# Expert weights with two neighbouring rows to a partition

## Chip, cores and metric

One core of one Trainium2 chip runs the whole program. The metric is the device time of one execution in microseconds (us). The kernel before takes 1276.35 us (median of 3 runs, 1276.34 to 1277.07).

## What is computed

A hybrid layer on 256 tokens and 16 meta tokens of width 1024, all in float32: a layer norm, an attention branch and a state-space branch, gates, an output projection, a second layer norm, a mixture of 32 experts (each token goes to its 4 best), and a last layer norm. The change lies in the experts:

```python
t = h.reshape(-1, dm)
logits = (t @ w_router + b_router).astype(jnp.float32)
top_v, top_i = lax.top_k(logits, TOP_K)
top_w = jax.nn.softmax(top_v, axis=-1)
comb = jnp.einsum('tk,tke->te', top_w, jax.nn.one_hot(top_i, N_EXPERTS, dtype=jnp.float32))
out = jnp.zeros(t.shape, jnp.float32)
for e in range(N_EXPERTS):
    gate = jnp.minimum(t @ w_gate[e] + b_gate[e], SWIGLU_LIMIT)
    up = jnp.clip(t @ w_up[e] + b_up[e], -SWIGLU_LIMIT, SWIGLU_LIMIT)
    act = (up + 1.0) * gate * jax.nn.sigmoid(SWIGLU_ALPHA * gate)
    out = out + comb[:, e:e + 1] * (act @ w_down[e] + b_down[e])
```

Each of `w_gate[e]`, `w_up[e]` and `w_down[e]` is a 1024 x 1024 matrix of 4 MiB, so the experts' weights are 384 MiB, and each is read once.

## The kernel before

The front (up to about 280 us) computes the norm, the two branches, the gates and the router. The experts follow in 16 pairs. For a pair, `gather` picks up to 64 tokens of each of the two experts by a product with a 0/1 matrix (`gather_mm`, line 908: the normed tokens `z1` are the stationary operand), and `affine` (line 848) puts the first norm's gain and bias on the result, which becomes `XT`, 8 tiles of 128 features. `gate_up` (line 1003) multiplies `XT` with the gate and up matrices, 64 columns of the array for each half of the output. `activate` makes the activation, `act_T` (line 1033) transposes it 128 features at a time into `aT`, and `down` (line 1041) multiplies with `w_down` for both experts side by side. `combine` (line 1057) adds the pair's result to the 256 tokens.

A weight matrix comes in quarters of 256 rows, 1 MiB each. `expert_load` (line 705) puts a quarter into a slot of 128 partitions x 2048 floats. Partition p of it takes row p and row 128 + p of the quarter: two pieces of 4096 B, 512 KiB apart in memory. `part_load` (line 701) loads the last two quarters of `w_down` in halves. There are 21 slots of 1 MiB in all for them; `homes` lists which load takes which.

The orders of PE (TensorE) and SP (which issues the loads) are the program's own, written out by hand; the other engines' orders come from a scheduler outside the stretches marked by hand. A load is issued when the slot that it takes has been read for the last time, so SP waits for PE, and PE waits for the transfers. In the front, rows of small parameters are loaded one above the other (`prow`, `prow2`) and transposed by PE into columns (`pcol`, `pcol2`), so that each partition has its feature's gain and bias.

A branch for experts with over 64 tokens (from line 1118 on) isn't taken with these inputs.

Of the kernel before, what the change touches and what calls it, by code (L numbers as in the profile page):

```python
# [9 lines left out]
F32 = mybir.dt.float32  # L10
# [4 lines left out]
AF = mybir.ActivationFunctionType  # L15
ALU = mybir.AluOpType
# [4 lines left out]
P = 128  # L21
D = 1024
KD = D // P
SEQ = 256
# [24 lines left out]
def hybrid_trunk_kernel(ctx: ExitStack, tc: tile.TileContext, x, meta, ln_in_g, ln_in_b, w_in, b_f,  # L49
# [3 lines left out]
    nc = tc.nc  # L53
    V, S, G, TE = nc.vector, nc.scalar, nc.gpsimd, nc.tensor

    def bc(ap, axis, n):
        a = ap.unsqueeze(axis)
        shape = list(a.shape)
        shape[axis] = n
        return a.broadcast_to(shape)  # L60
# [5 lines left out]
    keep = ctx.enter_context(tc.tile_pool(name="keep", bufs=1))  # L66
# [5 lines left out]
    sp = scan.enter_context(tc.tile_pool(name="sp", bufs=1, side="right"))  # L72
# [6 lines left out]
    def pst(cols, dt=F32, rows=P):  # L79
        t = ps.tile([P, 512], F32, name="ps", tag="ps")  # L80
        return t[:rows, :cols]
# [5 lines left out]
    ident = const.tile([P, P], F32, name="ident")  # L87
    make_identity(nc, ident)
    R_ARE, R_AIM, R_L1G, R_L1B, R_L2G, R_L2B, NROW = 16, 32, 48, 56, 64, 72, 80
    R_BGLU, R_D, R_BF, NROW2 = 0, 4, 8, 9  # L90
    prow0 = sp.tile([P, P], F32, name="prow0", tag="y", bufs=1)
    prow = sp.tile([P, P], F32, name="prow")
    prow2 = sp.tile([P, P], F32, name="prow2", tag="ya", bufs=1)
    ldt = sp.tile([16, 2], F32, name="ldt")

    def slab(src, kt):
# [27 lines left out]
    G.memset(prow2[:NROW2], 0.0)  # L124
    nc.sync.dma_start(prow2[R_BGLU:R_BGLU + 4], b_glu.rearrange("l (k p) -> (l k) p", p=P))
    nc.sync.dma_start(prow2[R_D:R_D + 4], ssm_d.rearrange("l (q g) c -> (l q) (g c)", g=8))
    nc.sync.dma_start(prow2[R_BF:R_BF + 1].rearrange("o (a b) -> o a b", b=32)[:, :, :NH], bc(b_f, 1, 4))
    ctt = ap_.tile([P, 2, 4, NS], F32, name="ctt", tag="vmz")
    ct = [ctt[:, i] for i in range(2)]
# [66 lines left out]
    pcol0 = sp.tile([P, 16], F32, name="pcol0")  # L196
    pcol = keep.tile([P, NROW], F32, name="pcol")
    pcol2 = keep.tile([P, 16], F32, name="pcol2")
    hT = fk.tile([P, KD, T], F32, name="hT", tag="hT")

    def col(r, n=1):
        return pcol[:, r:r + n]
# [18 lines left out]
    with tc.manual_schedule(engines={ENG.DVE, ENG.Activation, ENG.Pool}):  # L221
        for t_ in (wfp, bz, Mz, qA, kA):
            G.memset(t_, 0.0)
        G.tensor_scalar(prow[0:16].rearrange("j (g p) -> j g p", g=2), bc(ldt, 2, NS), 1.0, 1.0,
                        op0=ALU.mult, op1=ALU.mult)
        pp = pst(16)
# [15 lines left out]
        for n in range(2):  # L242
# [3 lines left out]
                            op0=ALU.mult, op1=ALU.add)  # L246
        for k in range(KD):
            pt = pst(T)
# [8 lines left out]
        pt = project(wu, 0, 0, T)  # L257
        pp = pst(NROW)
# [3 lines left out]
    pp = pst(NROW2)  # L262
    TE.transpose(pp, prow2[:NROW2], ident[:NROW2, :NROW2])
    S.copy(pcol2[:, :NROW2], pp)
    with tc.issue_after(xn.ins):
        mark = u_tile(1)
    with tc.issue_after(mark.ins):
# [117 lines left out]
    for i in range(2):  # L385
# [4 lines left out]
        pt = pst(512)  # L390
# [307 lines left out]

    home = homes()

    def part_load(t_, w, e, qtr, k):
        r = 256 * qtr + 128 * k
        nc.sync.dma_start(t_[:, k], w[0, e, r:r + 128])

    def expert_load(w, e, qtr, load=True):
        key = (w.tensor.name, e, qtr)
        if key in ready:
            return ready.pop(key)
        pool, tag = home[nload[0]]
        nload[0] += 1  # L710
        t_ = pools[pool].tile([P, 2048], F32, name="w", tag=tag).rearrange("p (k n) -> p k n", n=D)
        if load:
            nc.sync.dma_start(t_, w[0, e, qtr * 256:qtr * 256 + 256].rearrange("(k p) n -> p k n", p=P))
        return t_

    def prefetch(n):
# [128 lines left out]
    XT = xy[:, 0]  # L845
    Ysb = xy[:, 1].rearrange("p k n -> p (k n)")

    def affine(k, out_, in_):
        if k % 2:
            V.tensor_scalar(out_, in_, col(R_L1G + k), col(R_L1B + k), op0=ALU.mult, op1=ALU.add)  # L850
        else:
            S.activation(out_, in_, AF.Identity, scale=col(R_L1G + k), bias=col(R_L1B + k))  # L852

    def transposed(i):
        z1T[i] = xy[:, 1] if i else fk.tile([P, KD, P], F32, name="z1T", tag="y2T")
# [51 lines left out]

    def gather_mm(pts, sel, i):
        for k in range(KD):
            TE.matmul(pts[k // 4][:, (k % 4) * P:(k % 4 + 1) * P], z1[:, i, k * P:(k + 1) * P],  # L910
                      sel[:, i].rearrange("p e s -> p (e s)"), start=i == 0 and k % 4 == 0, stop=i == 1,
                      skip_group_check=True)

# [119 lines left out]
    def act_T(up):  # L1033
        pt = px.tile([P, 512], F32, name="px", tag="px")
        for j in range(4):
            TE.transpose(pt[:, j * P:(j + 1) * P], up[:, j * P:(j + 1) * P], ident)  # L1036
        aT = mp.tile([P, 4, 2, CAP], F32, name="aT", tag="aT", bufs=2)
        S.copy(aT.rearrange("p j h s -> p (j h s)"), pt)  # L1038
        return aT
# [78 lines left out]
    with tc.If(anyc > CAP):  # L1118
        free = [s_ for s_ in slots if s_ != ("keep", "gate1")]
        for s_ in home[-8:]:  # L1120
            free.remove(s_)
        free.sort(key=lambda s_: ("wC", "fk", "wB", "wA").index(s_[0]))

        def slot(n):
            pool, tag = free[n]
            return pools[pool].tile([P, 2048], F32, name="w", tag=tag)

        h1Td = slot(0).rearrange("p (k t) -> p k t", k=KD)
        for k in range(KD):
            pt = px.tile([P, 512], F32, name="px", tag="px")  # L1130
            for i in range(2):
                TE.transpose(pt[:, i * P:(i + 1) * P], z1[:, i, k * P:(k + 1) * P], ident)
            affine(k, h1Td[:, k], pt[:, :SEQ])
        with tc.For_i(0, NE, 1) as e:
            ce = nc.values_load(cnti[0:1, bass.ds(e, 1)], min_val=0, max_val=SEQ)
            with tc.If(ce > CAP):
                def weights_of(w, n):
                    ts = []
                    for qtr in range(4):
                        ts.append(slot(n + qtr).rearrange("p (k n) -> p k n", n=D))  # L1140
                        nc.sync.dma_start(ts[-1], w[0, bass.ds(e, 1), qtr * 256:qtr * 256 + 256]
                                          .rearrange("o (k p) n -> p (o k) n", p=P))
                    return ts

                scr = slot(1)
                a, sg, br, bu = scr[:, 0:512], scr[:, 512:1024], scr[0:1, 1024:], scr[32:33, 1024:]
                nc.sync.dma_start(br, b_gate[0, bass.ds(e, 1), :])
                nc.sync.dma_start(bu, b_up[0, bass.ds(e, 1), :])
                aT = slot(2).rearrange("p (k t) -> p k t", k=KD)
                wg_e, wu_e = weights_of(w_gate, 3), weights_of(w_up, 7)  # L1150
                for i in range(2):
                    for n in range(2):
                        ns = slice(n * 512, n * 512 + 512)
                        pts = []
                        for ws, bb_, r, tag in ((wg_e, br, 0, "pg"), (wu_e, bu, 32, "pu")):
                            pt = pg.tile([P, 512], F32, name=tag, tag=tag)
                            TE.matmul(pt, ones[r:r + 1, 0:P], bb_[:, ns], start=True, stop=False)
                            for k in range(KD):
                                TE.matmul(pt, h1Td[:, k, i * P:(i + 1) * P], ws[k // 2][:, k % 2, ns],
                                          start=False, stop=k == KD - 1)  # L1160
                            pts.append(pt)
                        V.tensor_scalar_min(a, pts[0], 7.0)
                        S.activation(sg, a, AF.Sigmoid, scale=1.702)
                        V.tensor_mul(sg, sg, a)
                        V.tensor_scalar(a, pts[1], 7.0, -7.0, op0=ALU.min, op1=ALU.max)
                        V.scalar_tensor_tensor(a, a, 1.0, sg, op0=ALU.add, op1=ALU.mult)
                        pt = px.tile([P, 512], F32, name="px", tag="px")
                        for j in range(4):
                            TE.transpose(pt[:, j * P:(j + 1) * P], a[:, j * P:(j + 1) * P], ident)
                        V.tensor_copy(aT[:, 4 * n:4 * n + 4, i * P:(i + 1) * P],  # L1170
                                      pt.rearrange("p (k t) -> p k t", k=4))
                wd_e = weights_of(w_down, 7)
                for i in range(2):
                    for n in range(2):
                        ns = slice(n * 512, n * 512 + 512)
                        pt = px.tile([P, 512], F32, name="px", tag="px")
                        for k in range(KD):
                            TE.matmul(pt, aT[:, k, i * P:(i + 1) * P], wd_e[k // 2][:, k % 2, ns],
                                      start=k == 0, stop=k == KD - 1)
                        V.scalar_tensor_tensor(acc[:, i, ns], pt, over[:, i, bass.ds(e, 1)], acc[:, i, ns],  # L1180
                                               op0=ALU.mult, op1=ALU.add)
# [81 lines left out]
```

## Time and profile before

| | us |
|---|---|
| median of 3 runs | 1276.35 |
| the profiled execution | 1274.92 |
| its span, from the first to the last instruction | 1273.2 |
| PE (matmul) busy | 1175.0 (92%) |
| PE weight loads busy | 573.8 (45%) |
| DVE busy | 328.8 (26%) |
| ACT busy | 169.1 (13%) |
| bytes moved by DMA | 433.09 MB, 340 GB/s over the span |

Busy time is the union of an engine's instructions. Matmuls are pipelined and their ends are modelled, so 92% for PE isn't 92% of its peak. The mean of 340 GB/s hides two stages: the front, which moves less, and the experts, where the loads run on without a break.

### The profile page before, as it was taken

The numbers are of one execution on the slowest core, as the hardware profiler recorded it, in microseconds if no ns is written. First come the engines' busy times: TensorE is split into PE (matmuls) and PEld (weight loads), VectorE is DVE, ScalarE is ACT, GpSimd is POOL, SyncE is SP. The second block draws the span as 40 slices with busy tenths as digits, with TensorE's granted clock in tenths as the row PEclk, the third lists the DMA queues.
The fourth block names the chain that finished last, engine by engine and source line by source line (L and its number), as shares of the span: only waits on it lengthen the run. The fifth ranks groups of instructions, "written<-read, shape, count | busy, mean of one in ns | idle before, by whom it ended". The sixth has DMA issues, their size and how long they took to land. (4 is left out here: it accounts for less than half of the span.)

```text
span 1273.2 us, 13451 instructions
## 1 busy us (share of the span) xinstructions
PE 1175.0 (92%) x5508; PEld 573.8 (45%) x5509; DVE 328.8 (26%) x784; ACT 169.1 (13%) x380; POOL 58.7 (5%) x115
## 2 busy tenths in 40 slices
PE   4889999989999999999999999999999999999965
PEld 2777888653434343344434343533434242424221
DVE  3969410241141212021111212121211111111103
ACT  2357201020101010010101010110101010101010
POOL 3324200000000000000000000000000000000001
PEclk9999999989989999999999999999999999999988
DMA  7651399459978999999999999999999999999970
GB/s 155 168 120 47 131 268 350 190 184 410 369 309 355 409 410 409 410 408 409 408 409 409 409 409 409 409 409 409 408 409 409 409 409 409 409 409 409 409 293 33
DMA packets 124507, 433.09 MB, mean 340 GB/s; under 512 B 14162, under 2 KB 14506, under 8 KB 124442
## 3 DMA queue, kind: packets, MB, share of 16 engines
q1 hardware_dynamic: 124010, 431.66, 88.4%
q8 instruction: 45, 0.74, 0.2%
q10 hardware_dynamic: 432, 0.52, 0.1%
q14 instruction: 20, 0.16, 0.0%
HBM read 431.11 MB, written 1.05 MB: 339 GB/s over the span
## 5 line engine op out<-in xcount | busy, mean ns | idle before, releaser
L1050 PE MATMUL Yp<-w,aT 128*64 128x512 f32 x1024 | 242.6, 606 | 10.9 <-PEq L1118 5.8
L1015 PE MATMUL pg<-w,xy 128*64 128x512 f32 x1024 | 239.7, 595 | 4.9 <-DMA w<-in_w_gate_dram 4.5
L1015 PE MATMUL pu<-w,xy 128*64 128x512 f32 x1024 | 231.5, 597 | 8.8 <-DMA w<-in_w_up_dram 8.4
L1050 PEld LDWEIGHTS Yp<-w,aT 128*64 128x64 f32 x1024 | 105.2, 139 | 134.4 <-issue 117.5
L1015 PEld LDWEIGHTS pg<-w,xy 128*64 128x64 f32 x1024 | 85.8, 137 | 145.7 <-issue 124.6
L1015 PEld LDWEIGHTS pu<-w,xy 128*64 128x64 f32 x1024 | 68.7, 136 | 168.6 <-issue 133.4
L210 PE MATMUL ps<-hT,w 128*128 128x256 f32 (+1 forms) x512 | 119.7, 393 | 2.8 <-ACT pr L587 2.8
L210 PEld LDWEIGHTS ps<-hT,w 128*128 128x128 f32 x512 | 98.3, 194 | 19.8 <-ACT pr L587 3.1
L1026 DVE TENSOR_SCALAR pg<-pg 128x512 f32<-128x512 f32 x32 | 22.4, 700 | 249.0 <-PE pg L1019 249.0
L1027 ACT ACTIVATE ups<-pg 128x512 f32<-128x512 f32 x32 | 19.1, 597 | 466.9 <-DVE pg L1026 466.9
L1029 DVE TENSOR_SCALAR pu<-pu 128x512 f32<-128x512 f32 x32 | 22.4, 700 | 208.3 <-PE pu L1019 208.3
L1053 DVE COPY xy<-Yp 128x512 f32<-128x512 f32 x16 | 11.1, 692 | 248.5 <-PE Yp L1050 248.5
L1061 PE MATMUL px<-xy,selT 128*128 128x512 f32 x120 | 61.2, 635 | 2.9 <-DVE acc L1062 2.9
L910 PE MATMUL px<-sel,z 128*128 128x128 f32 x480 | 57.6, 278 | 0.6 <-DVE sel L915 0.6
L910 PEld LDWEIGHTS px<-sel,z 128*128 128x128 f32 x480 | 55.8, 192 | 1.2 <-ACT aT L1038 0.8
L1213 POOL TENSOR_TENSOR acc<-acc,gb 128x512 f32<-128x512 f32 (+1 forms) x2 | 2.0, 994 | 1103.5 <-ACT acc L1211 1103.5
L1062 DVE TENSOR_TENSOR acc<-acc,px 128x512 f32<-128x512 f32 x60 | 39.8, 683 | 13.6 <-PE px L1061 13.6
L1054 ACT COPY xy<-Yp 128x512 f32<-128x512 f32 x16 | 9.4, 586 | 244.9 <-PE Yp L1050 244.9
L1061 PEld LDWEIGHTS px<-xy,selT 128*128 128x128 f32 x120 | 21.0, 195 | 43.6 <-issue 22.1
L1038 ACT COPY aT<-px 128x512 f32<-128x512 f32 x32 | 18.8, 587 | 127.5 <-PE px L1036 127.5
L850 DVE TENSOR_SCALAR xy<-px,pcol 128x128 f32<-128x128 f32 x60 | 23.6, 409 | 42.7 <-ACT xy L852 40.9
L1019 PE MATMUL pg<-bias,ident 32*64 32x512 f32 x128 | 34.3, 612 | 0.0
(349 smaller groups left out, 803.8 us busy)
## 6 DMA issues: line engine op xcount, KB each, us to landing
w<-in_w_gate_dram SPq DMA_DIRECT2D x128, 1024.0 KB, 13.0
w<-in_w_up_dram SPq DMA_DIRECT2D x128, 1024.0 KB, 18.3
w<-in_w_down_dram SPq DMA_DIRECT2D x126, 1024.0 KB, 18.3
w<-in_w_in_dram SPq DMA_DIRECT2D x16, 1024.0 KB, 16.2
w<-in_w_o_dram SPq DMA_DIRECT2D x4, 1024.0 KB
w<-in_w_up_a_dram SPq DMA_DIRECT2D x2, 1024.0 KB
w<-in_w_up_b_dram SPq DMA_DIRECT2D x2, 1024.0 KB
w<-in_w_down_dram SPq DMA_DIRECT2D x4, 512.0 KB, 15.7
```

What stands on the lines that cost most here:

```text
L210: TE.matmul(pt, w[k][:, j * P:(j + 1) * P], hT[:, k, n0:n1], start=k == 0, stop=k == KD - 1)
L850: V.tensor_scalar(out_, in_, col(R_L1G + k), col(R_L1B + k), op0=ALU.mult, op1=ALU.add)
L910: TE.matmul(pts[k // 4][:, (k % 4) * P:(k % 4 + 1) * P], z1[:, i, k * P:(k + 1) * P], sel[:, i].rearrange("p e s -> p (e s)"), start=i == ...
L1015: TE.matmul(pt[64 * n:64 * n + 64], XT[:, kk, c0:c0 + CAP], wt[:, k, n * 512:n * 512 + 512], start=kk == 0, stop=False, skip_group_check=True)
L1019: TE.matmul(pt[64 * n:64 * n + 64], ident[bs, NE * j + e:NE * j + e + 1].broadcast_to([NE, CAP]), bias[bs, n * 512:n * 512 + 512], start=F ...
L1026: V.tensor_scalar_min(pgt, pgt, 7.0)
L1027: S.activation(up, pgt, AF.Sigmoid, scale=1.702)
L1029: V.tensor_scalar(put, put, 7.0, -7.0, op0=ALU.min, op1=ALU.max)
L1038: S.copy(aT.rearrange("p j h s -> p (j h s)"), pt)
L1050: TE.matmul(Yp[n][64 * g:64 * g + 64], aTs[g][:, j, half], wd[g][:, k, n * 512:n * 512 + 512], start=qtr == 0 and k == 0, stop=qtr == 3 an ...
L1061: TE.matmul(pt, selT[:, i * P:(i + 1) * P], Ysb[:, ns], start=True, stop=True)
L1062: V.tensor_add(acc[:, i, ns], acc[:, i, ns], pt)
```

## The change

A slot now holds two neighbouring rows to a partition: partition p takes rows 2p and 2p + 1 of the quarter, 8192 B in one piece. So tile k of `XT` and of `aT` has to hold the features 256 (k // 2) + k % 2 + 2p. `paired(k)` gives that slice, of stride 2, and it is now the stationary operand in `gather_mm` and `act_T`, where 128 neighbouring columns stood before. `affine` needs gain and bias in the new order: two more small loads (`prowP`), two small transposes and a copy make `pcolP`. In the branch that isn't taken the old order is kept (`natural=True`).

```diff
+    prowP = sp.tile([8, 256], F32, name="prowP")
...
     nc.sync.dma_start(prow2[R_D:R_D + 4], ssm_d.rearrange("l (q g) c -> (l q) (g c)", g=8))
+    for j, a in enumerate((ln1_g, ln1_b)):
+        nc.sync.dma_start(prowP[4 * j:4 * j + 4], a.rearrange("l (q n) -> (l q) n", n=256))
     nc.sync.dma_start(prow2[R_BF:R_BF + 1].rearrange("o (a b) -> o a b", b=32)[:, :, :NH], bc(b_f, 1, 4))
...
+    pcolP = keep.tile([P, 16], F32, name="pcolP")
...
     S.copy(pcol2[:, :NROW2], pp)
+    pp = pst(16)
+    for k in range(2):
+        TE.transpose(pp[:, 8 * k:8 * k + 8], prowP[:, k::2], ident[:8, :8])
+    S.copy(pcolP, pp)
...
     def part_load(t_, w, e, qtr, k):
-        r = 256 * qtr + 128 * k
-        nc.sync.dma_start(t_[:, k], w[0, e, r:r + 128])
+        nc.sync.dma_start(t_[:, k], w[0, e, 256 * qtr:256 * qtr + 256].rearrange("(p k) n -> k p n", k=2)[k])
...
         if load:
-            nc.sync.dma_start(t_, w[0, e, qtr * 256:qtr * 256 + 256].rearrange("(k p) n -> p k n", p=P))
+            nc.sync.dma_start(t_, w[0, e, qtr * 256:qtr * 256 + 256].rearrange("(p k) n -> p k n", k=2))
...
-    def affine(k, out_, in_):
+    def paired(k):
+
+        return slice(256 * (k // 2) + k % 2, 256 * (k // 2) + 256, 2)
+
+    def affine(k, out_, in_, natural=False):
+        if natural:
+            g_, b_ = col(R_L1G + k), col(R_L1B + k)
+        else:
+            c = 8 * (k % 2) + k // 2
+            g_, b_ = pcolP[:, c:c + 1], pcolP[:, c + 4:c + 5]
         if k % 2:
-            V.tensor_scalar(out_, in_, col(R_L1G + k), col(R_L1B + k), op0=ALU.mult, op1=ALU.add)
+            V.tensor_scalar(out_, in_, g_, b_, op0=ALU.mult, op1=ALU.add)
         else:
-            S.activation(out_, in_, AF.Identity, scale=col(R_L1G + k), bias=col(R_L1B + k))
+            S.activation(out_, in_, AF.Identity, scale=g_, bias=b_)
...
     def gather_mm(pts, sel, i):
         for k in range(KD):
-            TE.matmul(pts[k // 4][:, (k % 4) * P:(k % 4 + 1) * P], z1[:, i, k * P:(k + 1) * P],
+            TE.matmul(pts[k // 4][:, (k % 4) * P:(k % 4 + 1) * P], z1[:, i, paired(k)],
...
-            TE.transpose(pt[:, j * P:(j + 1) * P], up[:, j * P:(j + 1) * P], ident)
+            TE.transpose(pt[:, j * P:(j + 1) * P], up[:, paired(j)], ident)
```

No instruction of the old program changes its place. On SP, among the experts, a pair's loads stand before as pieces of 2 x 1024 floats to a partition:

```order
L713 DMA w<-in_w_gate_dram 128x2x1024 x4
L713 DMA w<-in_w_up_dram 128x2x1024 x4
L713 DMA w<-in_w_gate_dram 128x2x1024 x4
L713 DMA w<-in_w_up_dram 128x2x1024 x4
L713 DMA w<-in_w_down_dram 128x2x1024 x8
```

and now in the same order, as one piece of 2048 floats:

```order
L721 DMA w<-in_w_gate_dram 128x2048 x4
L721 DMA w<-in_w_up_dram 128x2048 x4
L721 DMA w<-in_w_gate_dram 128x2048 x4
L721 DMA w<-in_w_up_dram 128x2048 x4
L721 DMA w<-in_w_down_dram 128x2048 x8
```

Only the shape differs. On SP in the front, between the small parameter loads (`prow_90` is `prow2`) and the first loads of the state-space branch, there stands before:

```order
L125 DMA prow_90<-in_b_glu_dram 4x128
L126 DMA prow_90<-in_ssm_d_dram 4x128
L127 DMA prow_90<-in_b_f_dram 1x4x8
L131 DMA ctt<-in_ssm_c_re_dram 128x4x64
L131 DMA ctt<-in_ssm_c_im_dram 128x4x64
```

and now:

```order
L126 DMA prow_90<-in_b_glu_dram 4x128
L127 DMA prow_90<-in_ssm_d_dram 4x128
L129 DMA prowP<-in_ln_g_dram 4x256
L129 DMA prowP<-in_ln_b_dram 4x256
L130 DMA prow_90<-in_b_f_dram 1x4x8
L134 DMA ctt<-in_ssm_c_re_dram 128x4x64
L134 DMA ctt<-in_ssm_c_im_dram 128x4x64
```

So everything from `b_f` on is issued two loads later. On PE, after the first projection of the front, there stands before:

```order
L210 MATMUL ps<-hT,w 128x272 x8
L259 MATMUL ps<-ident,prow 128x80
L263 MATMUL ps<-ident,prow_90 128x9
L210 MATMUL ps<-hT,w 128x272 x8
L392 MATMUL ps<-ident,cz 128x128 x8
```

and now:

```order
L214 MATMUL ps<-hT,w 128x272 x8
L263 MATMUL ps<-ident,prow 128x80
L267 MATMUL ps<-ident,prow_90 128x9
L271 MATMUL ps<-ident,prowP 128x8 x2
L214 MATMUL ps<-hT,w 128x272 x8
L400 MATMUL ps<-ident,cz 128x128 x8
```

Two small transposes come in ahead of the second projection.

## Rows read from the trace of the kernel before

**Rows 1.** The page: span, PE's busy time, and clock and DMA in 40 slices.

```profile
span 1273.2 us, 13451 instructions
...
PEclk9999999989989999999999999999999999999988
DMA  7651399459978999999999999999999999999970
GB/s 155 168 120 47 131 268 350 190 184 410 369 309 355 409 410 409 410 408 409 408 409 409 409 409 409 409 409 409 408 409 409 409 409 409 409 409 409 409 293 33
```

**Rows 2.** Windows, one per expert pair: start:end us, engines' busy us, PEclk, DMA share, GB/s.

```profile
408.60:466.20 57.60, 55.84 (x261) 22.75 (x259) 11.12 (x19) 5.05 (x10) 0.00 (x0) 1.00 1.03 409
...
523.80:583.20 59.40, 57.64 (x262) 25.79 (x260) 11.31 (x20) 5.05 (x10) 0.00 (x0) 0.97 1.03 409
...
872.60:930.40 57.80, 56.03 (x262) 22.73 (x260) 11.11 (x19) 5.05 (x10) 0.00 (x0) 1.00 1.03 409
930.40:991.80 61.40, 57.19 (x262) 21.77 (x260) 11.11 (x19) 5.05 (x10) 0.00 (x0) 1.00 1.03 409
...
1114.90:1177.60 62.70, 57.49 (x261) 21.45 (x260) 10.75 (x18) 5.05 (x10) 0.00 (x0) 1.00 1.03 409
...
930.40:1177.60 247.20, 229.22 (x1035) 86.07 (x1033) 44.09 (x75) 20.20 (x40) 0.00 (x0) 1.00 1.03 409
408.60:1222.00 813.40, 776.92 (x3543) 313.75 (x3539) 151.46 (x257) 69.76 (x137) 0.00 (x0) 1.00 1.03 409
```

**Rows 3.** Waits, whole run: engine line <- releaser: us, times, longest.

```profile
PEld pu L1015 <- DMA w<-in_w_up_dram: 33.7, 33, 1.5
```

**Rows 4.** Waits from 930 us to the end.

```profile
PEld pu L1015 <- DMA w<-in_w_up_dram: 31.6, 29, 1.5
```

**Rows 5.** Timeline, PE in a late pair: start us, us, instruction, idle before.

```profile
1006.61 1.94 PE L1015 MATMUL pu<-w,xy 128*64 128x512 f32 x8 [0.62 <-DMA w<-in_w_up_dram]
```

**Rows 6.** Waits of SP, the queue that issues the loads, whole run.

```profile
SPq L713 <- PE pg L1015: 179.2, 92, 20.5
SPq L713 <- PE Yp L1050: 152.4, 78, 13.7
```

**Rows 7.** Windows in the front and in the experts, columns as in rows 2.

```profile
28.00:32.00 4.00, 4.00 (x17) 3.07 (x17) 0.97 (x8) 1.05 (x2) 0.00 (x0) 1.00 1.04 161
39.00:43.00 4.00, 3.86 (x12) 3.22 (x13) 4.00 (x21) 0.89 (x2) 0.53 (x1) 0.58 1.05 397
40.00:41.00 1.00, 1.00 (x5) 0.77 (x4) 1.00 (x6) 0.59 (x1) 0.00 (x0) 0.50 1.07 406
42.00:43.00 1.00, 1.00 (x5) 0.79 (x4) 1.00 (x7) 0.00 (x0) 0.00 (x0) 0.81 1.06 408
500.00:504.00 4.00, 4.00 (x24) 1.52 (x21) 0.71 (x2) 0.11 (x1) 0.00 (x0) 1.00 1.02 409
```

**Rows 8.** Timeline, SP in the front.

```profile
23.43 25.66 SPq L103 DMA_DIRECT2D w<-in_w_in_dram  x6
```

**Rows 9.** Timeline, PE's weight loads at a pair's transposes and gather.

```profile
735.15 0.42 PEld L1036 LDWEIGHTS px<-ident,ups 128*128 128x128 f32 x4 [0.81 <-issue]
735.54 3.76 PEld L910 LDWEIGHTS px<-sel,z 128*128 128x128 f32 x32
```

**Rows 10.** Timeline, PE in the front: a matmul whose moving operand has stride 2.

```profile
100.45 0.49 PE L507 MATMUL ps<-uT,Mz 128*128 128x128 f32 x2
100.78 0.62 PE L210 MATMUL ps<-hT,w 128*128 128x272 f32 x2
```

**Rows 11.** Timeline, SP and PE where the front's new instructions come in.

```profile
18.23 0.30 SPq L126 DMA_DIRECT2D prow<-in_ssm_d_dram  x1
18.57 0.74 SPq L127 DMA_DIRECT2D prow<-in_b_f_dram  x1
...
30.89 0.22 PE L263 MATMUL ps<-ident,prow 9*128 9x9 f32 x1
...
38.05 0.63 PE L392 MATMUL ps<-ident,cz 128*128 128x128 f32 x4 [3.07 <-DVE cz L388]
```

More of the change, by code (lines that the diff above doesn't have):

```diff
@@ L1132, in hybrid_trunk_kernel @@
                 TE.transpose(pt[:, i * P:(i + 1) * P], z1[:, i, k * P:(k + 1) * P], ident)
-            affine(k, h1Td[:, k], pt[:, :SEQ])
+            affine(k, h1Td[:, k], pt[:, :SEQ], natural=True)
         with tc.For_i(0, NE, 1) as e:
```

## The prediction

> **What bounds the kernel now.** I read the page first: from about 400 us on the DMA engines are full in every slice and move 409 GB/s, until the loads end in the last slices [rows 1]. Then I cut that stretch at the starts of the expert pairs [rows 2]. Two regimes show. Nine pairs, from 408 to 930 us (three of them stand there), take 57.6 to 57.8 us each, or 59.4 where the granted clock dips to 0.97; PE is idle for 1.8 us of such a pair. The four pairs after that (first and last stand there) take 61.4 to 62.7 us with the same instructions. The waits say why: of 33.7 us in which the up product's weight loads waited for a transfer, 31.6 lie after 930 us [rows 3, 4], in bites of about 0.6 us, one per 1 MiB quarter [rows 5].
>
> So DMA is the limit throughout, and the first half only lives on stock. A pair needs 24 MiB, 25.17 MB, which at 409 GB/s takes 61.5 us; PE needs 57.6. At 408 us the 21 slots are full, PE eats 3.9 us of lead per pair, and after nine pairs the lead is gone. SP's own waits are for PE to give slots back [rows 6]: there is always a load in the queue. The end is set by when the last byte comes. Two prices follow:
> - DMA is full for 813.4 us [rows 2]. One per cent of rate is worth 8.1 us.
> - PE caps a gain. The four pairs from 930 us take 247.2 us where PE alone needs 4 x 57.6 = 230.4, that is 16.8 us; the last pair adds 0 to 3.9 in the same way; one clock dip more costs about 1.8. I take 18 us. It is reached when the rate is up by 2.3% (813.4 x (1 - 409/r) = 18 gives 418 GB/s).
>
> The profiled execution took 1274.92 us, 1.72 more than its span, and the median is 1.43 above it; the sums below are differences, made on the trace and put on 1276.35.
>
> **The loads, the main term.** 384 quarters of 1 MiB are loaded as before, in the same order; 382 of them as 128 pieces of 8192 B instead of 256 of 4096, while the last two, which come as halves, keep pieces of 4096 B. No row shows weights in pieces of 8192 B. The question is what a piece costs besides its bytes, and the trace has pieces of two sizes: between 23 and 49 us only slices of `w_in` are in flight [rows 8], in pieces of 2048 B. While they run without a break, they move 397 GB/s over 4 us, 406 and 408 in its two undisturbed microseconds [rows 7], against 409 for 4096 B. One piece thus holds an engine for 16 x 2048 B / 407 GB/s = 80.5 ns, and one of 4096 B for 160.2. Doubling the piece cost 79.7 ns, almost exactly its bytes. Going on in a line, 8192 B hold it for 160.2 + 2 x 79.7 = 319.6 ns, which is 410 GB/s: a gain of 0.25%, 2 us. From the 408 alone it is 1 us. From the whole 4 us at 397 it is 82.5 ns, then 315.6, 415.3 GB/s, 1.5% and 12 us, but that window holds some slow pieces that have to do with their rows. The other bound is a loss: the same 2048 B pieces of `w_in` crawl at 161 GB/s from 28 to 32 us with the engines just as full [rows 7], so which rows are read can cost far more than the piece. Against that, the new piece reads two neighbouring rows instead of two 512 KiB apart. I take 1 us gained: rate looks like a ceiling per byte near 409, which pieces of 2048 B already touch.
>
> **The stationary operands of stride 2.** 512 weight loads of the gathers and 128 of `act_T` now read every second float. Dense, they follow each other every 0.117 us (3.76 us for 32) [rows 9], with a matmul of 128 columns between, so a load that is much slower shows at once in PE's pace. No row has a stationary operand of stride 2. The nearest has a moving one: `uT[:, q, NMETA::2]`, two matmuls whose successor starts 0.33 us after the first, three steps of 0.11, no longer than the dense step [rows 10]. I take 0. The upper bound is a doubling, 40 loads x 0.117 = 4.7 us per pair. Even without that row, cover is there: PE has 61.5 - 57.6 = 3.9 us per pair to spare as long as DMA is the limit. Only the first gather (32 loads, ahead of the experts) has no cover; doubled it costs 3.7 us.
>
> [...]
>
> **The rest.** In the front SP issues two small loads more, ahead of `b_f` and all that follows; neighbours take 0.30 and 0.74 us [rows 11], so the state-space inputs and the six `w_in` loads come 0.6 us later at the least, 1.5 at the most. PE has two small transposes more, each like the 0.22 us one before it, and ACT one small copy. Behind them PE waits 3.07 us for DVE [rows 11], which hides the transposes; of the later loads I take 0.3 us through, between 0 and 1.5. A delay of the front delays slots, and so the end, one for one. The operands of `affine` only change their tile: 0. Sum: -1 + 0 + 0.3, that is 1275.6 us.
>
> **Rivals.**
> - *Each piece has a price of its own* (faster). If the 397 GB/s is the truer rate of 2048 B, the end comes 12 us earlier, at 1264; if the price is larger still, PE's cap sets 1258. For it: a window of 4 us is longer than one of 1 us, and the DMA engines' share over 1.00 shows packets that overlap at their edges. Against: in its undisturbed parts the small piece is as fast as the large one. [...]
> - *The strided load is slower* (slower). It decides from 18 us / 608 loads = 30 ns on 117, where PE's pace passes DMA's. A doubling costs 608 x 0.117 = 71 us against the 18 of cover, plus 3.7 ahead: 1333. For it: nothing covers a load in the gather. Against: [rows 10].
> - *The new row order reads slower* (slower). Over 0.3% it shows, each per cent is 8.1 us: 1284 at one. For it, the 161 GB/s row; against it, larger neighbouring pieces.
> - *The pieces are cut to 4096 B again*: then nothing changes but the front, 1276.7, the same class as my forecast.
>
> **Chances.** A measurement of this kernel can tell about 0.2%, 2.55 us. No change, by a ceiling per byte or cut pieces: 0.60, 1273.8 to 1278.9. A price per piece: 0.26, most of it between 1260 and 1273, down to 1258 where PE caps it. Slower: 0.14, 0.08 for the strided load and 0.06 for the order of rows. The range runs from 1257, PE's cap with 1 us to spare, to 1284, one per cent of lost rate; beyond it are mostly the larger prices of a strided load.
>
> **What would show it.** Right: pairs after 930 us still at 61.4 us and 409 GB/s, some 49,000 packets fewer (382 x 128), the 0.62 us waits still there, the gather's 32 loads in 3.8 us. A price per piece: over 410 GB/s in the windows, late pairs at 57.6 to 60 us, waits for `w_up` gone. A strided load: 32 of them in over 4.7 us (3.76 + 32 x 0.03) and early pairs over 59 us. Rows in a bad order: under 408 GB/s and pairs over 62 us from the start of the shortage, which then comes before 930 us. What would make me wrong most cheaply is that 1 us windows misled me on the rate of 2048 B.

## The result, and the profile after

| | before | after |
|---|---|---|
| median, us | 1276.71 (4 runs, 1276.34 to 1279.84) | 1256.23 (4 runs, 1255.58 to 1258.40) |
| the profiled execution, us | 1274.92 | 1256.27 |
| its span, us | 1273.2 | 1254.5 |
| DMA rate in the experts, GB/s | 409 | 421 |
| DMA packets | 124507 | 75628 |

The changed kernel is faster: the ratio is 0.9837, 95% interval 0.9818 to 0.9857. I had forecast no change, and the time lies 0.8 us below my range.

The page of the kernel after, its span, clock and DMA in 40 slices, against [rows 1]:

```profile
span 1254.5 us, 13457 instructions
...
PEclk9999999989989999999999999999999999999988
DMA  7642299549878999999999999999999999999960
GB/s 151 177 110 59 105 252 356 239 167 363 368 309 339 424 421 421 421 421 421 421 421 421 421 420 421 421 421 421 421 420 422 421 421 420 421 421 421 422 248 34
DMA packets 75628, 433.09 MB, mean 345 GB/s; under 512 B 14171, under 2 KB 14523, under 8 KB 26667
```

The same bytes move in 48,879 packets fewer, and every full slice of the expert stage shows 420 to 424 GB/s where [rows 1] had 408 to 410. DMA is as full as before, but faster. Now cut the stage by pairs, as in [rows 2] (start:end us, busy time of PE, weight loads, DVE, ACT and POOL, granted clock, DMA share, GB/s). The first of the 13 pairs after 410 us, the one that starts where the loads had run short before, the last, and all 13 together:

```profile
410.40:468.30 57.90, 56.13 (x261) 23.09 (x259) 11.17 (x19) 5.05 (x10) 0.00 (x0) 1.00 1.01 422
...
932.00:990.00 58.00, 56.24 (x262) 23.20 (x260) 11.17 (x19) 5.05 (x10) 0.00 (x0) 1.00 1.02 422
...
1106.10:1164.10 58.00, 56.23 (x261) 22.43 (x259) 10.80 (x18) 5.05 (x10) 0.00 (x0) 1.00 1.01 421
...
410.40:1164.10 753.70, 730.75 (x3357) 298.63 (x3355) 144.85 (x246) 65.63 (x130) 0.00 (x0) 1.00 1.01 421
```

All 13 pairs take 57.9 to 58.0 us, late ones too; the second regime, 61.4 to 62.7 us, is gone. A pair's 25.17 MB take 59.8 us at 421 GB/s, so PE still eats the stock of full slots, but by 1.8 us per pair instead of 3.9, and it lasts to the end. The waits of the weight loads (engine, line, releaser: us, times, longest) show it; this was 33.7 us in [rows 3]:

```profile
PEld pu L1032 <- DMA w<-in_w_up_dram: 3.9, 8, 0.8
```

The expert products themselves wait for no weights any more; before, they waited 12.9 us (8.4 for `w_up`, 4.5 for `w_gate`).

The end of the loads shows what is late now. Before, PE reached the branch for full experts at 1225 us and stood still for 5.8 and 4.3 us, until 1236, when the last weights had just come (timeline of PE of the kernel before; DMA in the window at its end):

```profile
1224.37 0.66 PE L1036 MATMUL px<-ident,ups 128*128 128x128 f32 x4
1230.80 1.09 PE L1050 MATMUL Yp<-w,aT 128*64 128x512 f32 x1 [5.77 <-PEq L1118]
1236.18 4.47 PE L1050 MATMUL Yp<-w,aT 128*64 128x512 f32 x10 [4.29 <-issue]
```

```profile
1234.00:1236.00 2.00, 0.00 (x0) 0.00 (x0) 0.00 (x0) 0.00 (x0) 0.00 (x0) 0.50 0.15 59
```

In the kernel after PE passes the same place in one gap of 8.7 us (timeline of PE), which four kernels further down repeat at 8.4 to 9.0 us wherever it falls. The loads end during it (DMA in the last window):

```profile
1207.49 0.74 PE L1053 MATMUL px<-ident,ups 128*128 128x128 f32 x4
1216.95 5.75 PE L1067 MATMUL Yp<-w,aT 128*64 128x512 f32 x14 [8.72 <-issue]
```

```profile
1212.00:1214.00 2.00, 0.00 (x0) 0.00 (x0) 0.00 (x0) 0.00 (x0) 0.00 (x0) 0.50 0.18 72
```

What fills this gap the trace doesn't say ("issue"), but the loads don't end it. So PE sets the end; the loads are over some 3 us earlier. Of the 18.7 us by which the span is shorter, 13.5 are gained by the start of the last pair (1177.6 to 1164.1) and 5.2 after it.

### The profile page after: what moved, and what is told of

Read it like the earlier page. It is cut to its first block, busy times and chain, and to the rows that moved or that the text cites. A ratio compares the mean times of both kernels' runs of the same rounds, so it can differ in the third digit from the quotient of the medians.

```text
span 1254.5 us, 13457 instructions
## 1 busy us (share of the span) xinstructions
PE 1171.1 (93%) x5510; PEld 575.4 (46%) x5511; DVE 330.0 (26%) x784; ACT 169.2 (13%) x381; POOL 58.6 (5%) x115
## 2 busy tenths in 40 slices
DMA packets 75628, 433.09 MB, mean 345 GB/s; under 512 B 14171, under 2 KB 14523, under 8 KB 26667
## 5 line engine op out<-in xcount | busy, mean ns | idle before, releaser
L1067 PE MATMUL Yp<-w,aT 128*64 128x512 f32 x1024 | 239.0, 598 | 9.5 <-issue 8.7
L1032 PE MATMUL pu<-w,xy 128*64 128x512 f32 x1024 | 227.0, 595 | 0.0
L1067 PEld LDWEIGHTS Yp<-w,aT 128*64 128x64 f32 x1024 | 97.4, 138 | 137.1 <-issue 123.9
L927 PE MATMUL px<-sel,z 128*128 128x128 f32 x480 | 59.8, 283 | 0.6 <-DVE sel L932 0.6
L927 PEld LDWEIGHTS px<-sel,z 128*128 128x128 f32 x480 | 58.6, 197 | 0.8 <-ACT aT L1055 0.8
L867 DVE TENSOR_SCALAR xy<-px,pcolP 128x128 f32<-128x128 f32 x60 | 23.7, 410 | 45.3 <-ACT xy L869 43.4
L1036 PE MATMUL pu<-bias,ident 32*64 32x512 f32 x128 | 34.3, 612 | 0.0
```

The costliest lines, as they stand in the source:

```text
L867: V.tensor_scalar(out_, in_, g_, b_, op0=ALU.mult, op1=ALU.add)
L1032: TE.matmul(pt[64 * n:64 * n + 64], XT[:, kk, c0:c0 + CAP], wt[:, k, n * 512:n * 512 + 512], start=kk == 0, stop=False, skip_group_check=True)
L1036: TE.matmul(pt[64 * n:64 * n + 64], ident[bs, NE * j + e:NE * j + e + 1].broadcast_to([NE, CAP]), bias[bs, n * 512:n * 512 + 512], start=F ...
L1067: TE.matmul(Yp[n][64 * g:64 * g + 64], aTs[g][:, j, half], wd[g][:, k, n * 512:n * 512 + 512], start=qtr == 0 and k == 0, stop=qtr == 3 an ...
```

## Experiments: which part of the change, and which property of the load

My theory after the result: a piece has a price besides its bytes. At 409 GB/s a piece of 4096 B holds one of 16 engines for 16 x 4096 / 409 = 160.2 ns; at 421 a piece of 8192 B holds it for 311.3. The rivals: the order of the rows (two neighbours to a partition) is what reads faster; or my own reading of `w_in`, by which rate is a ceiling per byte up to 4096 B and something else happens at 8192.

**Pieces of 2048 B, same rows.** `e2_rows_2k` keeps the row order of after and halves the columns of each load:

```diff
-            nc.sync.dma_start(t_, w[0, e, qtr * 256:qtr * 256 + 256].rearrange("(p k) n -> p k n", k=2))
+            src = w[0, e, qtr * 256:qtr * 256 + 256].rearrange("(p k) n -> p k n", k=2)
+            for c in (0, 512):
+                nc.sync.dma_start(t_[:, :, c:c + 512], src[:, :, c:c + 512])
```

> The changed kernel with one edit: each quarter is loaded by two DMAs, one for each half of the columns, so a partition gets the same two neighbouring rows in four pieces of 2048 B. **Price per piece**: 4096 B took an engine 16 x 4096 / 409 = 160.2 ns before, 8192 B take 16 x 8192 / 421 = 311.3 ns now. Doubling cost 151.1 ns, so a piece costs 9.1 ns besides its bytes. 2048 B then take 75.6 + 9.1 = 84.7 ns, which is 387 GB/s; the 813.4 us in which DMA was full become 813.4 x 409 / 387 = 860, and the time 1276.4 + 46 = 1322 us. **Row order** (two neighbouring rows to a partition read faster, whatever the pieces): 421 GB/s, 1256 us. **Ceiling per byte up to 4096 B**, as my prediction read it from w_in (408 GB/s at 2048 B), and something else at 8192 B: 406 to 409 GB/s, 1276 to 1282 us.

Measured: 1324.49 us (1324.02 to 1324.80), 1.0375 times the kernel before, interval 1.0353 to 1.0396. A window of the stage, and the chain that ended last by engine:

```profile
420.00:1260.00 840.00, 803.27 (x3438) 315.56 (x3434) 150.19 (x254) 66.44 (x132) 0.00 (x0) 0.99 1.05 387
```

```profile
DMA 67%; PE 26%; DVE 4%; issue 1%; ACT 1%; SPq 1%; POOL 0%; DVEq 0%; ACTq 0%; POOLq 0%
```

The rate is 387 GB/s and the time within 2.5 us of the theory's; row order and my ceiling fall. The three sizes lie on a line. One MiB, 64 KiB for each engine, takes it 2490.7 ns at 421, 2563.8 at 409 and 2709.5 at 387 GB/s; 8 pieces more cost 73.1 ns, 16 more cost 145.7, which is 9.1 ns a piece both times. The rates are read to 1 GB/s, which leaves up to 0.8 ns open in these figures. This kernel also issues twice as many loads, so a price for each load is included in the second step; by the equality it is at most some 20 ns for an engine, which can't be told from nothing here.

**Pieces of 4096 B, other rows.** `e1_rows_4k` takes the even or the odd rows of a half of 512, so neighbouring partitions read 8192 B apart and the two pieces of a partition lie 1 MiB apart:

```diff
...
-            nc.sync.dma_start(t_, w[0, e, qtr * 256:qtr * 256 + 256].rearrange("(p k) n -> p k n", k=2))
+            h, j = 512 * (qtr // 2), qtr % 2
+            nc.sync.dma_start(t_, w[0, e, h:h + 512].rearrange("(k p j) n -> j p k n", p=P, j=2)[j])
...
-        return slice(256 * (k // 2) + k % 2, 256 * (k // 2) + 256, 2)
+        c = 512 * (k // 4) + 256 * (k % 2)
+        return slice(c + k // 2 % 2, c + 256, 2)
...
```

> The changed kernel with pieces of 4096 B again: a quarter takes the even or the odd rows of a half of 512 rows, so partition p gets rows 2p and 256 + 2p (or the odd ones), two pieces 1 MiB apart, and neighbouring partitions read 8192 B apart instead of 4096 as before. Operands stay strided, with the features in that order. **Price per piece**: 409 GB/s, as before, late pairs at 61.4 to 62.7 us, 1276 to 1277 us. **Row order** as a cause at all (it is not the size of the piece): a rate other than 409; if a pitch of 8192 B between the pieces of neighbouring partitions is what helps, 421 GB/s and 1256 us; if reading every second row hurts, under 405 GB/s and over 1284 us.

Measured: 1278.04 us, ratio 1.0013 (1.0002 to 1.0024). Window:

```profile
1000.00:1060.00 60.00, 57.07 (x254) 25.86 (x252) 10.48 (x18) 5.04 (x10) 0.00 (x0) 0.97 1.03 409
```

409 GB/s again: with pieces of 4096 B the new order of rows and the strided operands gain nothing. A load fills the same 8192 B of a partition here, before and after; only the pieces in memory differ. The 0.1% over the kernel before is one to two us that I don't split further.

**The loads of before under the operands of after.** In `e3_old_loads` the weight rows don't match the order of the features.

```diff
...
-            nc.sync.dma_start(t_, w[0, e, qtr * 256:qtr * 256 + 256].rearrange("(p k) n -> p k n", k=2))
+            nc.sync.dma_start(t_, w[0, e, qtr * 256:qtr * 256 + 256].rearrange("(k p) n -> p k n", p=P))
```

> The changed kernel with the loads of before (two pieces of 4096 B to a partition, 512 KiB apart) and the strided operands of after. The weight rows then don't match the order of the features; the work is otherwise the same. **Loads carry all of the gain**: 409 GB/s, late pairs at 61.4 to 62.7 us, 1276 to 1278 us; the strided operands cost 0.4 us per pair while PE sets the pace (58.0 instead of 57.6) and nothing at the end, since DMA's limit covers them. **Something else in the change carries a part** (the new order of operands, the front): clearly under 1274 us. If the stride weren't covered: 1276.4 + 16 x 0.4 = 1283 us.

Measured: 1277.20 us, ratio 1.0010 (0.9997 to 1.0024), no difference that can be measured. Window:

```profile
1000.00:1060.00 60.00, 55.97 (x254) 22.18 (x254) 11.16 (x19) 5.04 (x10) 0.00 (x0) 1.00 1.03 409
```

The loads carry all of the gain, and DMA's limit covers the stride as long as it is the limit.

**The loads of after under dense operands.** In `e4_dense` the features don't match the weight rows.

```diff
     def paired(k):
 
-        return slice(256 * (k // 2) + k % 2, 256 * (k // 2) + 256, 2)
+        return slice(k * P, (k + 1) * P)
```

> The changed kernel with the new loads of 8192 B, but dense stationary operands as before (paired(k) gives 128 neighbouring columns). The features then don't match the order of the weight rows; the work is otherwise the same. **PE is the cap now, and the stride costs 0.4 us per pair**: 421 GB/s as in after, pairs at 57.6 us instead of 58.0, 1256.2 - 16 x 0.4 = 1249.8 us. **DMA still sets the end at 421 GB/s**: 1256 us, with waits for weights in the last pairs. **Stride is free** and 58.0 has another reason: pairs stay at 58.0, 1256 us with no waits for weights.

Measured: 1256.36 us, ratio 0.9850 (0.9822 to 0.9878), the time of after. None of the three had it whole. Windows: an undisturbed pair, a disturbed one, 1 us within that one, another disturbed pair, and all 13 pairs:

```profile
408.90:466.60 57.70, 55.93 (x262) 22.85 (x260) 11.12 (x19) 5.05 (x10) 0.00 (x0) 1.00 1.01 422
466.60:525.90 59.30, 57.53 (x261) 25.13 (x259) 11.21 (x20) 5.05 (x10) 0.00 (x0) 0.97 1.01 421
511.00:512.00 1.00, 1.00 (x4) 0.37 (x4) 0.00 (x0) 0.18 (x1) 0.00 (x0) 0.50 1.04 434
640.90:700.20 59.30, 57.53 (x261) 22.02 (x259) 11.31 (x20) 5.05 (x10) 0.00 (x0) 0.97 1.01 421
408.90:1163.80 754.90, 731.94 (x3357) 305.45 (x3355) 144.19 (x246) 65.64 (x130) 0.00 (x0) 0.99 1.01 421
```

The pairs are shorter, as the first theory said, but four of 13 take 59.3 us at a granted clock of 0.97, where the kernel after has none. Such a dip is 3 to 4 us at a granted clock of 0.50 (the window of 1 us above; the whole pair shows 0.97). The 13 take 754.9 us here and 753.7 there. What the dense operands save in these two executions, the clock takes back.

## Experiments: can both costs be avoided, and what does a larger stride cost

If the four dips were chance, a kernel with dense operands and matching rows would beat both. The new order can be made once where the data are written: when `z1` is copied out of PSUM, and when the activation writes `ups`. `e5_paired_once` does both, `e7_z1_once` the first alone (`act_T` stays strided), `e8_ups_ordered` the second alone (the gather stays strided).

```diff
+    def paired(ap):
+        return ap.rearrange("p (a q j) -> p a j q", a=2, j=2)
+    def ordered(ap):
+        return ap.rearrange("p (a j q) -> p a j q", a=2, j=2)
...
-                S.copy(z1[:, i, n * 512:n * 512 + 512], po[i][n])
+                S.copy(ordered(z1[:, i, n * 512:n * 512 + 512]), paired(po[i][n]))
...
-            TE.matmul(pts[k // 4][:, (k % 4) * P:(k % 4 + 1) * P], z1[:, i, paired(k)],
+            TE.matmul(pts[k // 4][:, (k % 4) * P:(k % 4 + 1) * P], z1[:, i, k * P:(k + 1) * P],
...
-        S.activation(up, pgt, AF.Sigmoid, scale=1.702)
-        V.tensor_mul(up, up, pgt)
-        V.tensor_scalar(put, put, 7.0, -7.0, op0=ALU.min, op1=ALU.max)
-        V.scalar_tensor_tensor(up, put, 1.0, up, op0=ALU.add, op1=ALU.mult)
+        S.activation(ordered(up), paired(pgt), AF.Sigmoid, scale=1.702)
+        V.tensor_mul(ordered(up), ordered(up), paired(pgt))
+        V.tensor_scalar(ordered(pgt), paired(put), 7.0, -7.0, op0=ALU.min, op1=ALU.max)
+        V.scalar_tensor_tensor(up, pgt, 1.0, up, op0=ALU.add, op1=ALU.mult)
...
-            TE.transpose(pt[:, j * P:(j + 1) * P], up[:, paired(j)], ident)
+            TE.transpose(pt[:, j * P:(j + 1) * P], up[:, j * P:(j + 1) * P], ident)
```

> Loads of 8192 B as in after, but the new order is made once where the data are written, not where they are read: z1 is copied out of PSUM in paired order, and the activation writes ups in paired order, so that all stationary operands are 128 neighbouring columns again, and rows and features match. The dense run before this one had no strided operands, pairs of 57.6 us and four stretches at a lower granted clock, each costing 1.7 us, and came out at 1256.4. **The clock takes back what the stride cost** (a PE that does the same in 57.6 us is slowed down about every fourth pair): 57.2 to 57.6 us in most pairs, 59.3 in four, 1256 us. **The dips of that run were chance**: 57.6 in all pairs, 1250 us. **The permuting writes cost something**: over 1258, with longer waits for ups or XT in the gather's stretch.

> As e5_paired_once for z1 alone: the gather reads dense columns, while act_T still reads every second float, so only 8 of the 40 strided loads of a pair are left. The stride's cost by rows of after: 0.30 us per pair in the gather (2 x 0.15), 0.14 x 2 in act_T, of which about 0.1 us is in PE's pace. **A dense gather is what brings the clock down**: pairs of 57.7 us and three or four dips to 59.4, 1255 to 1257 us. **Any bit of slack is enough to keep the clock up**: 57.7 us throughout, 1256.2 - 16 x 0.3 = 1251.4 us, which beats both kernels.

> The other half of e5_paired_once: the activation writes ups in paired order, so act_T reads dense columns, while the gather's 32 loads stay strided. **The gather decides on the clock**: pairs of 57.9 us and no dip among the experts, 1256.2 - 16 x 0.1 = 1254.6 us. **act_T decides**: 57.9 and three or four dips, 1259 to 1261 us.

Measured, with the pairs as the windows of each trace show them:

| | median, us | ratio to before (interval) | undisturbed pair, us | pairs with a dip, of 13 | the 13 pairs, us |
|---|---|---|---|---|---|
| `e4_dense` | 1256.36 | 0.9850 (0.9822 to 0.9878) | 57.6 | 4 | 754.9 |
| `e5_paired_once` | 1257.12 | 0.9848 (0.9828 to 0.9868) | 57.6 | 4 | 755.4 |
| `e7_z1_once` | 1256.68 | 0.9842 (0.9827 to 0.9857) | 57.8 | 2 | 753.9 |
| `e8_ups_ordered` | 1256.09 | 0.9848 (0.9828 to 0.9868) | 57.8 | 2 | 754.1 |
| after | 1256.23 | 0.9837 (0.9818 to 0.9857) | 58.0 | 0 | 753.7 |

One disturbed pair of `e5_paired_once`, `e7_z1_once` and `e8_ups_ordered` in turn, each with its 13 pairs (windows, columns as above):

```profile
699.90:759.30 59.40, 57.63 (x262) 25.95 (x260) 11.22 (x20) 5.04 (x10) 0.00 (x0) 0.97 1.01 421
410.40:1165.80 755.40, 732.45 (x3359) 297.66 (x3357) 144.42 (x247) 65.57 (x130) 0.00 (x0) 0.99 1.01 421
```

```profile
701.00:760.50 59.50, 57.73 (x263) 22.14 (x261) 11.39 (x20) 5.04 (x10) 0.00 (x0) 0.97 1.01 421
412.30:1166.20 753.90, 730.95 (x3357) 300.42 (x3355) 143.93 (x246) 65.57 (x130) 0.00 (x0) 1.00 1.01 421
```

```profile
582.80:642.30 59.50, 57.73 (x263) 22.05 (x261) 11.41 (x20) 5.04 (x10) 0.00 (x0) 0.97 1.01 421
409.50:1163.60 754.10, 731.15 (x3358) 295.76 (x3356) 144.79 (x246) 65.57 (x130) 0.00 (x0) 1.00 1.01 421
```

The five kernels can't be told apart by time, and the 13 pairs lie within 1.7 us. A dip costs 1.7 us, and in these traces each 0.2 us that a pair is shorter goes with two dips more in 13 pairs: 57.6 + 4 x 1.7 / 13 = 58.1, 57.8 + 2 x 1.7 / 13 = 58.1, and 58.0 without any. The counts are of one execution each, but the mean granted clock of every run agrees: 0.976 to 0.980 in the nine of the two dense kernels, 0.979 to 0.983 in the nine of the two half-strided ones, 0.981 to 0.984 in the four of after, where one dip takes 1.7 / 1254 = 0.0014. The dips lie between 43 and 49 us after the start of a pair (744 to 748 us, at 0.57, in the pair of `e5_paired_once` above), behind the gather and PE's wait of 1.4 us that follows it, when the second transposes and the products of `down` run. For `e7_z1_once` I had two theories, that a dense gather brings the clock down (three or four dips) and that any slack keeps it up (none); it had two, and so had `e8_ups_ordered` with its gather strided, so neither holds, nor does the split between gather and `act_T`. Each strided half costs 0.2 us per pair and goes with half of the dips gone. The permuting writes of `e5_paired_once` cost nothing that shows. That the 13 pairs come out even is shown; what rule the clock follows is not. Neither the stride nor slowness protects: `e2_rows_2k`, with the operands of after and 65 us per pair (25.17 MB at 387 GB/s), shows 0.97 from 800 to 860 us, 0.84 and 0.73 in the two windows of 4 us from 1208 us, and a mean clock of 0.978 to 0.980 over its runs; the next kernel dips too. None of these beats the kernel after. There was little to beat: its loads end some 3 us before PE goes on at 1217 us, and DMA is full almost to their end. So by the end of these loads the 1250 us that I had put for dense operands without dips were out of reach, and equal times alone say little about the clock; the 13 pairs do.

**Other rows at the same piece, and stride 4.** `e6_stride_4` takes the first or the last two of each four rows, 8192 B at a pitch of 16384:

```diff
...
-            nc.sync.dma_start(t_, w[0, e, qtr * 256:qtr * 256 + 256].rearrange("(p k) n -> p k n", k=2))
+            h, j = 512 * (qtr // 2), qtr % 2
+            nc.sync.dma_start(t_, w[0, e, h:h + 512].rearrange("(p j k) n -> j p k n", j=2, k=2)[j])
...
-        return slice(256 * (k // 2) + k % 2, 256 * (k // 2) + 256, 2)
+        return slice(512 * (k // 4) + k % 4, 512 * (k // 4) + 512, 4)
...
```

> Pieces of 8192 B as in after, but other rows: a quarter takes, of each four rows of a half of 512, the first two or the last two. So neighbouring partitions read 16384 B apart instead of 8192, and the stationary operands are columns 4 apart (16 B) instead of 2. **Price per piece, whatever the rows**: 421 GB/s, SP's queue and waits as in after. **Neighbouring pieces matter**: a rate other than 421. [...]

Measured: 1318.18 us, ratio 1.0316 (1.0290 to 1.0342); the runs lie at 1311.5 and 1311.6, with a mean granted clock of 0.982, and three times at 1318.2 to 1319.3, with 0.973 to 0.976; the profile is of the one at 1311.6, so single us mean nothing here. Two windows, 20 us within a pair and a whole pair:

```profile
430.00:450.00 20.00, 19.79 (x82) 6.15 (x80) 5.35 (x8) 0.60 (x1) 0.00 (x0) 1.00 1.02 423
...
544.50:606.10 61.60, 59.84 (x262) 26.83 (x260) 11.25 (x19) 5.05 (x10) 0.00 (x0) 1.00 1.00 409
```

While the loads run they run at 423 GB/s: the pitch of the rows doesn't matter at this size either. Over a pair it is 409, since PE now takes 61.6 us for it and the slots come free later; PE's weight loads wait 1.9 us in all for transfers between 408 and 1215 us, and the clock dips all the same: the pair from 667.6 to 730.9 us takes 63.3 us at 0.97, and the stage from 408 to 1160 us shows 0.99. The stride's price stands in the timeline of PE's weight loads (start us, busy us, count), stride 4, then stride 2 in the kernel after, against the dense loads in [rows 9]:

```profile
767.80 0.56 PEld L1055 LDWEIGHTS px<-ident,ups 128*128 128x128 f32 x4 [0.81 <-issue]
768.27 7.54 PEld L929 LDWEIGHTS px<-sel,z 128*128 128x128 f32 x32
```

```profile
737.11 0.56 PEld L1053 LDWEIGHTS px<-ident,ups 128*128 128x128 f32 x4 [0.81 <-issue]
737.58 3.91 PEld L927 LDWEIGHTS px<-sel,z 128*128 128x128 f32 x32
```

The gather's 32 loads take 3.76 us dense, 3.91 at stride 2 and 7.54 at stride 4. The last step, 3.6 us, is the whole of the longer pair (61.6 against 58.0). From stride 2 to stride 4 the loads double in the gather and there alone: `act_T`'s four take 0.42, 0.56 and 0.56 us, so they don't follow the same law; I leave that open.

## Why the prediction was wrong

**What bounds the kernel: right.** DMA was the limit, and a faster rate moved the end by what it should, up to where PE takes over. The two prices hold. From 409 to 421 GB/s the 813.4 us of [rows 2] would have shrunk by 23.2 us; PE's cap of 18 us is less, and the two profiled executions differ by 18.65 (the medians by 20.5). The cap's parts shifted a little: the nine pairs that PE paced before took 521.8 us, and the first nine of after take 521.6 (410.4 to 932.0), two dips fewer against 0.4 us of stride; the last pair and the end gave 5.2 us where I had allowed 0 to 3.9.

**The loads, the main term: this step failed.** I wrote that a piece costs "almost exactly its bytes", from microseconds of `w_in` at 406 and 408 GB/s [rows 7], and took 1 us. My two points left a piece 80.5 - 79.7 = 0.8 ns of its own. It costs 9.1 ns besides its bytes, 2.9% of rate at this size, and the rate that follows was worth 23.2 us, of which PE let 18.65 through, where I put 1. I had the right form, a line through two sizes, and gave it a bad point: in pieces of 2048 B the experts' weights run at 387 GB/s. The same windows of `w_in` in other traces show that a window of 1 us can't carry such a number. The windows from 39 to 43 us and within it, of the kernel after, then of `e2_rows_2k` (start:end, then the length; the last number is GB/s); the six loads of `w_in` are the same there and start 0.7 to 1.0 us later than before:

```profile
39.00:43.00 4.00, 3.63 (x14) 2.73 (x13) 4.00 (x21) 1.17 (x2) 0.53 (x1) 0.65 1.03 368
40.00:41.00 1.00, 1.00 (x6) 0.88 (x5) 1.00 (x7) 0.47 (x2) 0.30 (x1) 0.61 1.08 416
41.00:42.00 1.00, 1.00 (x3) 0.77 (x3) 1.00 (x5) 0.14 (x1) 0.00 (x0) 0.50 1.03 379
42.00:43.00 1.00, 1.00 (x3) 0.69 (x3) 1.00 (x6) 0.00 (x0) 0.00 (x0) 0.50 1.04 367
```

```profile
39.00:43.00 4.00, 3.63 (x12) 2.84 (x12) 4.00 (x21) 1.17 (x2) 0.52 (x1) 0.62 1.03 377
40.00:41.00 1.00, 1.00 (x5) 0.77 (x4) 1.00 (x7) 0.59 (x1) 0.00 (x0) 0.50 1.05 397
41.00:42.00 1.00, 1.00 (x4) 0.77 (x3) 1.00 (x6) 0.00 (x0) 0.00 (x0) 0.50 1.05 389
42.00:43.00 1.00, 1.00 (x3) 0.77 (x3) 1.00 (x5) 0.00 (x0) 0.00 (x0) 0.50 1.04 385
```

The single microseconds go from 367 to 416. The window of 4 us in [rows 7] had 397, which alone would have given 415 GB/s; the prediction named that as the other end and set it aside for the better-looking microseconds. To be nearer with it would have been luck: the same 4 us read 368 and 377 in the other two traces, which by the same line would have given 433 and 427. A difference of 3% was sought in a sample that scatters by more than 10%.

**The rival that won** is the first: a price for each piece, in the case that "if the price is larger still, PE's cap sets 1258". It came to 1256.2. I gave the whole rival 0.26: I weighed it against single windows and dropped it, though its form was the thing to take. Extrapolated to no price at all, the line of the three sizes (387, 409 and 421 GB/s) gives an estimate of 16 x 2048 / (84.7 - 9.1) = 433 GB/s, which no window of a whole pair shows.

**The strided operands.** Forecast 0, and the time shows 0, but not for my reasons alone. The loads are a little slower [rows 9], and a pair takes 58.0 us instead of 57.6. I had also misread [rows 10]: its 0.33 us hold two matmuls, 0.165 us each, and not three steps of 0.11, so the row was no evidence that stride 2 is free. Under DMA's limit the cover holds (`e3_old_loads`); at PE's limit fewer dips of the clock give the same back (`e4_dense`, `e5_paired_once`), which I had not forecast. The doubling that I took as the upper bound was an assumption that no row of before showed. The rival of a slower load decided from 30 ns per load. Measured are 0.4 us per pair, 10 ns for each of 40 loads, at stride 2; at stride 4 the gather's take (7.54 - 3.76) / 32 = 118 ns more, and that kernel came out slower, as the rival said.

**The other rivals.** The row order reads no slower and no faster (409 in `e1_rows_4k`, 423 in `e6_stride_4`, 421 in after). The pieces were not cut: 48,879 packets fewer, 382 x 128 is 48,896. **The front**: the first gate product starts at 282.2 us instead of 281.3. With the same front the six `w_in` loads start at 24.45 us in after and at 24.16 in `e2_rows_2k`; my 0.3 can't be told from that scatter.

**What I said would show it** did: over 410 GB/s in the windows, late pairs at 57.6 to 60 us, the waits for `w_up` down from 33.7 to 3.9 us. The cheapest way to be wrong that the prediction named, that windows of 1 us misled me on 2048 B, is what happened.

## What to carry to other kernels

Where DMA is the limit, ask how many pieces the bytes come in: on this chip 4096 B gave 409 GB/s and 8192 B gave 421, and a change in which rows share a partition is enough to double the piece. Take a rate for a small difference from windows of tens of us or from several traces, never from the best microsecond; and when a resource is nearly balanced with the next, work out the cap first, since it gave the size of this gain to within 1 us (18 against 18.65 on the profiled executions) while the rate was still unknown. In the gather a strided stationary operand was cheap at stride 2 (3.91 us for 32 loads against 3.76 dense) and took about twice the time at stride 4 (7.54 us).

## What the runs showed of the hardware

- An estimate from the rates at 2048, 4096 and 8192 B (387, 409, 421 GB/s) puts the price of a DMA piece besides its bytes at 9.1 ns of an engine at all three sizes, with neighbouring partitions' rows 4096 or 8192 B apart at 4096 B a piece, and 8192 or 16384 B apart at 8192 B. Twice as many loads of half the size (`e2_rows_2k`) cost nothing more that shows: 1324.49 us against the 1322 expected from the pieces alone.
- The granted clock dips to 0.50 for 3 to 4 us in some pairs, behind the gather where the windows show the place. Of five kernels that differ by 0.4 us per pair, none of 13 pairs had one at 58.0 us, two at 57.8 and four at 57.6, which leaves the same mean. It dipped with 61.6 us per pair too (`e6_stride_4`, 0.97 from 667.6 to 730.9 us) and with 65 us (`e2_rows_2k`, 0.97 from 800 to 860 us), so a slower PE doesn't keep it up, and what rule it follows stays open.
- SP's waits changed their name: in [rows 6] they are for PE, from 1000 to 1180 us too, and in the kernel after nearly all of that stretch are for earlier transfers:

```profile
SPq L721 <- DMA w<-in_w_gate_dram: 51.7, 24, 3.2
SPq L721 <- DMA w<-in_w_down_dram: 50.3, 24, 2.1
SPq L721 <- DMA w<-in_w_up_dram: 50.3, 24, 2.1
SPq L721 <- PE pu L1032: 1.0, 4, 0.3
```

That is 2.1 us for each of 72 loads, which take 2.5 us each (1 MiB at 421 GB/s): SP runs at the pace of the transfers. The wait is put down to whatever came last, so I read no more from it.
